# A hybrid decoder layer on one core: raw-weight tiles, the order of the experts, one expert's turn and the order of score products

## The chip, the cores and the metric

The kernel runs on one core of a Trainium2 chip. The metric is the device time of one execution in microseconds (us). TensorE, VectorE (DVE), ScalarE (ACT), GpSimd (POOL) and SyncE (SP, which issues most loads) each run their own list of instructions in order.

## The reference

One layer on 512 tokens of width 1024, all in f32: an input projection feeds four heads of chunked retention and eight heads of sliding-window attention; an output projection follows; then 32 experts, of which each token takes four; then a gated embedding and the last norm.

```python
hn = rmsnorm(h, g_mix_norm)
rq, rk, rv, rg, aq, ak, av = split_cols(hn @ w_in + b_in, IN_SIZES)
ret = silu(rg) * rmsnorm(retention(rq, rk, rv, positions), ret_norm_g)
att = sliding_window_attention(aq, ak, av, att_sinks, rel_bias_table)
h = h + concatenate([ret, att]) @ w_out
h = h + moe(rmsnorm(h, g_moe_norm), ...)   # per expert: clamped_swiglu(x @ w_up + b_up) @ w_down + b_down
gate = sigmoid(h @ w_ple_gate)
h = h + rmsnorm(gate * (p @ w_ple_proj), g_ple_norm)
return rmsnorm(h, g_final)
```

## The kernel before

**Weights.** All matrices of the later stages come as pieces of 1 MB (128 x 2048 f32), in one fixed list: w_out (4 pieces), then for each expert 8 pieces of w_up followed by the 4 pieces of w_down of the expert before it, then those of the end. A piece is loaded by SyncE into a raw tile taken from the list `free`, and a tile goes back there once its piece has been used or split. There are 12 raw tiles in three pools: `rawp` (3, there from the start), `raw2` (5, opened when attention and retention have been written down) and `raw3` (4, which first hold the mixed head outputs `mix` and come free tile by tile in the second half of the output projection). `next_piece` splits a piece into a high part `wh` on ScalarE (L150) and the rest `wl` on VectorE (L151), three tiles of each; a product of split operands takes three matmuls (`mm3`, L307 to L309). `whole_piece` uses a raw tile as it is.

**Stages.** Retention and attention run to about 212 us, woven into the products of the input projection (L315). Then the output projection goes over two halves of the columns and four token tiles in each (24 matmuls of 512 columns per tile and half, 192 in all), with transposes, router logits and top-4 after each tile (`route_tile`). Each token tile's normed rows `xn` go to the table xg in memory, from which every expert gathers its tokens (`gather`, L800). The expert stage follows from 297 to 1392 us.

**Experts.** They are sorted by how many tokens they have. The string `BIG` says for each rank whether it is handled big (L: up to 96 tokens, weights split, `up` at L847 and `down` at L928) or small (S: up to 64, weights straight from the raw tile, `up64` and `down64`, L864). Expert 0 and 1 are L. In the loop, the up products of expert e stand ahead of the down products of expert e - 1. The tokens of expert e + 1 are gathered two steps ahead, and turned (transposed on TensorE, copied by ScalarE into `xTh`: `prep` at L300, `prep64` at L815) right behind the up products of e, so ahead of the down products of e - 1. `act` computes the gated activation: Silu `sg` on ScalarE (L895), clamp and product on VectorE; `act_t` transposes it to `aTh`. `gated` scales the down result to `y`, and GpSimd scatters it into acc.

**Order.** A list scheduler orders each engine's instructions when the kernel is built, from the written order and its own estimates; `tc.issue_after` pins an instruction behind another.

Of the kernel before, what the change touches and what calls it, by code (L numbers as in the profile page):

```python
# [33 lines left out]
LIMIT = 7.0  # L34
S_MAX = float(ALPHA * LIMIT / (1.0 + math.exp(-ALPHA * LIMIT)))
CAP = 96
RAW1, RAW2, RAW3 = 3, 5, 4
FAR = 1000.0


# [3 lines left out]

BIG = [c == "L" for c in "LL" + "SLSLSLSLSLSLSLL" + "SLSLSLSLSLSLLLS"]
NBIG = sum(BIG)
RANK = [sum(BIG[:t]) if BIG[t] else NBIG + t - sum(BIG[:t]) for t in range(len(BIG))]
CAPS = 64  # L50
# [45 lines left out]
def hymba_kernel(ctx, tc, x, p, positions, rel_bias_table, g_mix_norm, w_in, b_in, ret_norm_g,  # L96
# [24 lines left out]
        return stack.enter_context(tc.tile_pool(name=name, bufs=bufs, reuse_waits="tile", **kw))  # L121

    const = pool(ctx, "const")
    rawp = pool(ctx, "rawp", RAW1)
    whp = pool(ctx, "whp", 3)
    wlp = pool(ctx, "wlp", 3)
    small = pool(ctx, "small", 3)
# [4 lines left out]


    R = SimpleNamespace(eid={})
    free = [rawp] * RAW1

    def raw_tile(dt=F32):
        pl_ = free.pop(0)
        return pl_.tile([P, 2048], dt, name="raw"), pl_

    def split(raw, parts=None, dst=None):
        if dst is None:
# [181 lines left out]

    px = ctx.enter_context(ExitStack())
    right = ctx.enter_context(ExitStack())
    raw3 = pool(ctx, "raw3", RAW3)
    mix = [raw3.tile([P, 2048], F32R, name="raw").rearrange("p (a k t) -> a p k t", a=2, k=KD) for _ in range(NT)]
    mm = pool(px, "mm", 2, PSUM)
    tp = pool(px, "tpp", 2, PSUM)  # L330
    sps = pool(px, "sps", 2, PSUM)
# [133 lines left out]
    def attention(nb):  # L465
        nk = 1 if nb == 0 else 2
        k0 = max(nb - 1, 0) * P
        o_sb = at2.tile([P, 512], F32, name="o_sb", bufs=1)
        o_ps = flat(oap.tile([P, 4, P], F32, name="o_ps")).rearrange("p (h d) -> p h d", d=64)
        sm = small.tile([P, 8], F32, name="sm")  # L470
        mx = small.tile([P, 8], F32, name="mx")
        nmx = small.tile([P, 8], F32, name="nmx")
        kvs = [slice(kv * 64, kv * 64 + 64) for kv in range(2)]
        for gp in range(2):

            s_ps = [sps.tile([P, 512], F32, name="s_ps").rearrange("p (a b) -> p a b", a=2) for _ in range(2)]
            for g in range(2):
                for kv, rows in enumerate(kvs):
                    nc.tensor.matmul(s_ps[kv][:, g, 0:nk * P], lhsT=aqT[rows, gp * 2 + g, nb * P:(nb + 1) * P],
                                     rhs=akT[rows, k0:k0 + nk * P], start=True, stop=True)  # L480
            for kv, rows in enumerate(kvs):
                h0 = kv * 4 + gp * 2
                h2_ = slice(h0, h0 + 2)
                s_sb = at2.tile([P, S], F32, name="s_sb").rearrange("p (a b) -> p a b", a=2)
                nc.vector.scalar_tensor_tensor(
                    s_sb[:, :, 0:nk * P], in0=s_ps[kv][:, :, 0:nk * P], scalar=0.125,
                    in1=band[:, h2_, 256 - nk * P:256], op0=ALU.mult, op1=ALU.add)
                nc.vector.tensor_reduce(out=mx[:, h2_], in_=s_sb[:, :, 0:nk * P], op=ALU.max, axis=AX.X)
# [124 lines left out]
    p1.close()  # L613


    raw2 = pool(right, "raw2", RAW2, side="right")
    rt = pool(right, "rt", side="right")
    free += [raw2] * RAW2

# [12 lines left out]
    for r0 in (0, 64):  # L632
        nc.gpsimd.memset(b_raw[r0:r0 + E, 0:1536], 0.0)
    nc.vector.scalar_tensor_tensor(R.bias, in0=b_hi[:, 0:1536].bitcast(F32), scalar=cst[:, C_SGN:C_SGN + 1],
                                   in1=b_raw[:, 0:1536], op0=ALU.mult, op1=ALU.add)
    state["limit"] = n_moe
    while free:
        prefetch()
# [99 lines left out]
    for c in range(2):  # L738
        cs = slice(c * 512, (c + 1) * 512)
        ws = {1: next_piece(), 0: next_piece()}  # L740
        for i in range(NT):
# [4 lines left out]
                mm3(ps, (mix[i][0][:, k, :], mix[i][1][:, k, :]), [kslice(w, k % 4) for w in ws[k // 4]],  # L746
                    k == order[0], k == order[-1])
            if c == 1:
                free.append(raw3)
                prefetch()  # L750
            nc.vector.tensor_tensor(out=h1[:, i, cs], in0=ps, in1=h1[:, i, cs], op=ALU.add)
            t = tp.tile([P, 4, P], F32, name="tp")
# [10 lines left out]
            if c == 0:  # L763
                nc.vector.tensor_copy(out=lg[:, i, :], in_=o)
            else:
                nc.vector.tensor_tensor(out=lg[:, i, :], in0=o, in1=lg[:, i, :], op=ALU.add)
                xn = tl.tile([P, D], F32, name="xn")
                for cc in range(2):
                    cs = slice(cc * 512, (cc + 1) * 512)
                    nc.gpsimd.tensor_tensor(out=xn[:, cs], in0=h1[:, i, cs], in1=g_moe[:, cs], op=ALU.mult)  # L770
                r = rstd(hs[i], None, 1)
                R.last_act = nc.scalar.activation(xn, xn, AF.Copy, scale=r)
                logits = tl.tile([P, E], F32, name="logits")
                nc.vector.scalar_tensor_tensor(logits, in0=lg[:, i, :], scalar=r, in1=b_rt, op0=ALU.mult, op1=ALU.add)
                nc.sync.dma_start(out=xg[tok, :], in_=xn)
                nc.sync.dma_start(out=acc[tok, :], in_=h1[:, i, :])
                route_tile(i, logits)


    def route(posm_ap, v_ap):  # L780
# [106 lines left out]

    def act(h):

        sg = R.sb.tile([P, FF], F32, name="sg", bufs=1)  # L890
        a = R.sb.tile([P, FF], F32, name="a", bufs=1)
        for v, h_ in enumerate(h):
            hv = h_.rearrange("p (c t) -> p c t", t=2)
            cs = slice(v * 512, (v + 1) * 512)
            nc.scalar.activation(sg[:, cs], hv[:, :, 0], AF.Silu, scale=ALPHA)  # L895
            nc.vector.tensor_scalar(a[:, cs], hv[:, :, 1], LIMIT + 1.0, 1.0 - LIMIT, op0=ALU.min, op1=ALU.max)  # L896
            R.act = nc.vector.scalar_tensor_tensor(a[:, cs], in0=sg[:, cs], scalar=S_MAX, in1=a[:, cs], op0=ALU.min,
                                                   op1=ALU.mult)
        return a

# [32 lines left out]
        return o  # L933

    def gated(o, gate):
        y = R.sb.tile([P, D], F32, name="y")
        nc.scalar.activation(y[:, 0:o.shape[1]], o, AF.Copy, scale=gate)  # L937
        return y

# [75 lines left out]

    def read_slots():

        tab = R.sb.tile([P, D], F32, name="y")[0:CAP, 0:8 * E].rearrange("p (k f) -> p k f", k=4)
        half = R.sb.tile([P, D], F32, name="y")[:, 0:E]
        for k in range(4):  # L1020
            nc.gpsimd.dma_start(out=tab[:, k, :], in_=slot_d[k].rearrange("(s e) c -> s (e c)", e=E))
        sums = slots.rearrange("p e c -> p (e c)")[0:CAP]
# [31 lines left out]
    for e in range(E + 1):  # L1054
        if e < E:
# [10 lines left out]
            if e == 0:  # L1066
                read_slots()
                static_gather(2)
            if e + 1 < E:
                with tc.issue_after(R.up_end.ins):  # L1070
                    xT = (prep if BIG[e + 1] else prep64)(xe[(e + 1) % 2])
        if e == E - 1:

            last = raw_tile()
# [16 lines left out]
        if e < E - 1:  # L1091
            with tc.issue_after(R.dn_mid.ins) if e else nullcontext():
                aT = act_t(a) if BIG[e] else act_t64(a)

    h2 = [t for _ in range(2) for t in raw_tile()[0].rearrange("p (a n) -> a p n", a=2)]
    proj = [t for _ in range(2) for t in raw_tile()[0].rearrange("p (a n) -> a p n", a=2)]
# [22 lines left out]
    with tc.If(any_v > 0), ExitStack() as sx:  # L1119
# [4 lines left out]
        for i in range(NT):  # L1124
            nc.gpsimd.dma_start(out=pos_d.rearrange("e p i -> p e i")[:, :, i], in_=posm[:, i, :])
            nc.gpsimd.dma_start(out=gate_d.rearrange("e p i -> p e i")[:, :, i], in_=gates[:, i, :])
        pe = ov.tile([P, NT], F32, name="pe")
        ge = ov.tile([P, NT], F32, name="ge")
        with tc.For_i(0, E, 1) as ev:
            n_e = nc.values_load(nblk[0:1, bass.ds(ev, 1)], min_val=0, max_val=NT)  # L1130
            nc.sync.dma_start(out=pe, in_=pos_d[bass.ds(ev, 1), :, :].rearrange("o p i -> p (o i)"))
# [2 lines left out]
            with tc.For_i(0, n_e, 1):  # L1134
# [7 lines left out]
                xd = R.sb.tile([P, D], F32, name="y")  # L1142
                nc.gpsimd.memset(xd, 0.0)
                gather(idx, xd, P)
                xTd = prep(xd)
# [32 lines left out]
    with tc.issue_after(ld.ins):  # L1178
        for _ in range(2):
            prefetch()  # L1180
    g_ple = bcast(ep2, g_ple_norm[0], D, "g_ple", nc.sync)
    g_fin = bcast(ep2, g_final, D, "g_fin", nc.sync)
    ws = [ws]
    free += [t[1] for t in (last, tmp, tf, tr)]
    hT = {}
    ss1 = {}

# [90 lines left out]
```

## Time and profile before

| | before |
|---|---|
| median of 3 runs | 1484.46 us (1481.01 to 1488.48) |
| profiled execution | 1485.38 us |
| its span | 1483.6 us |
| TensorE busy | 91% |
| VectorE busy | 56% |
| ScalarE busy | 46% |
| mean granted TensorE clock | 0.958 |
| memory traffic read | 447.26 MB |

The span is the traced part of the execution; 1.8 us lie around it. Busy shares are averages over stages that differ, so the text below goes by stage. A matmul's duration overlaps that of the next; its rate is read from the starts.

### The profile page before, as it was taken

To read this page: it belongs to the slowest core of one execution; us is meant where nothing else is said; L and a number is where in the kernel's file an instruction comes from. 1 tells how busy PE (TensorE), PEld (TensorE's weight loads), DVE (VectorE), ACT (ScalarE), POOL (GpSimd) and SP (SyncE) were. 2 spreads that over 40 slices of the span, in tenths; PEclk is the share of its full clock that TensorE was granted. 3 is DMA by queue.
4 is the path that set the end of the run, shared out by engine and by line. 5 is a ranking of instruction groups with operands and counts; after the bars stand their busy time and mean duration, and the time that the engine had idled before them with its cause. 6 is when DMAs were issued, how large, how long until landed. Compare 5 with 4: busy or idle time off the path is not lost. (4 is left out here: it accounts for less than half of the span.)

```text
span 1483.6 us, 16861 instructions
## 1 busy us (share of the span) xinstructions
PE 1351.3 (91%) x6090; PEld 907.1 (61%) x6091; DVE 830.1 (56%) x1005; ACT 677.7 (46%) x750; POOL 224.4 (15%) x238
## 2 busy tenths in 40 slices
PE   5999999588999999999999999999999999999885
PEld 4777777466657474655647657465655647675564
DVE  6637774776547263544637647354553726683356
ACT  5333443455536253543626535343452625573443
POOL 2213241474100000000000000000100000000023
PEclk9999999788999999999999999999999999999998
DMA  9332046667899999999999999999999999987511
GB/s 272 118 109 58 29 142 254 237 254 280 318 402 396 403 405 396 406 399 393 392 396 408 393 388 387 375 403 396 386 394 399 395 387 400 391 328 283 183 72 43
DMA packets 110427, 462.47 MB, mean 312 GB/s; under 512 B 10830, under 2 KB 29180, under 8 KB 77568
## 3 DMA queue, kind: packets, MB, share of 16 engines
q1 hardware_dynamic: 99584, 436.24, 74.8%
q0 software_dynamic: 10320, 24.52, 6.5%
q8 instruction: 49, 0.80, 0.2%
q10 hardware_dynamic: 432, 0.57, 0.1%
q14 instruction: 42, 0.34, 0.1%
HBM read 447.26 MB, written 18.73 MB: 314 GB/s over the span
## 5 line engine op out<-in xcount | busy, mean ns | idle before, releaser
L151 DVE TENSOR_TENSOR wl<-raw,wh 128x2048 fp32r<-128x2048 f32 (+2 forms) x243 | 530.2, 2222 | 151.8 <-ACT wh L150 143.8
L150 ACT ACTIVATE wh<-raw 128x2048 fp32r<-128x2048 f32 (+2 forms) x243 | 442.9, 1858 | 110.2 <-PE up L847 52.2
L864 PE MATMUL up<-raw,xTh 128*64 128x512 f32 x896 | 195.3, 594 | 0.0
L896 DVE TENSOR_SCALAR a<-up 128x512 f32<-128x512 f32 x50 | 32.9, 687 | 267.8 <-ACT sg L895 267.8
L847 PE MATMUL up<-wh,xTh 128*128 128x512 f32 x576 | 162.8, 405 | 9.2 <-ACT wh L150 7.8
L895 ACT ACTIVATE sg<-up 128x512 f32<-128x512 f32 x50 | 27.9, 595 | 297.0 <-issue 158.5
L847 PE MATMUL up<-wl,xTh 128*128 128x512 f32 x576 | 160.9, 401 | 2.2 <-DVE wl L151 2.2
L847 PE MATMUL up<-wh,xTl 128*128 128x512 f32 x576 | 161.0, 401 | 1.4 <-DVE xTl L292 1.4
L864 PEld LDWEIGHTS up<-raw,xTh 128*64 128x64 f32 x896 | 63.1, 137 | 124.6 <-issue 120.0
L847 PEld LDWEIGHTS up<-wh,xTh 128*128 128x128 f32 x576 | 108.7, 191 | 40.5 <-ACT wh L150 13.1
L847 PEld LDWEIGHTS up<-wl,xTh 128*128 128x128 f32 x576 | 109.0, 191 | 32.8 <-DVE wl L151 7.0
L847 PEld LDWEIGHTS up<-wh,xTl 128*128 128x128 f32 x576 | 109.8, 191 | 28.2 <-DVE xTl L292 1.8
L928 PE MATMUL dn<-wh,aTh 128*128 128x512 f32 x288 | 100.8, 434 | 23.8 <-ACT wh L150 23.8
L928 PE MATMUL dn<-wl,aTh 128*128 128x512 f32 x288 | 104.0, 446 | 15.9 <-DVE wl L151 15.9
L942 POOL DMA_INDIRECT acc<-y,slot_i x30 | 45.4, 1514 | 443.3 <-ACT y L937 434.8
L800 POOL DMA_INDIRECT xe<-xg,slot_i x30 | 31.9, 1064 | 485.9 <-PE dn L857 261.0
L864 PE MATMUL dn<-raw,aT 128*64 128x512 f32 x448 | 102.9, 598 | 0.0
L928 PE MATMUL dn<-wh,aTl 128*128 128x512 f32 x288 | 98.2, 425 | 0.0
L928 PEld LDWEIGHTS dn<-wh,aTh 128*128 128x128 f32 x288 | 59.4, 211 | 42.8 <-ACT wh L150 27.3
L928 PEld LDWEIGHTS dn<-wl,aTh 128*128 128x128 f32 x288 | 58.5, 212 | 35.5 <-DVE wl L151 23.1
L914 DVE SCALAR_TENSOR_TENSOR aTl<-tp,aTh 128x512 fp32r<-128x512 f32 x36 | 24.1, 689 | 90.2 <-ACT aTh L913 90.2
L928 PEld LDWEIGHTS dn<-wh,aTl 128*128 128x128 f32 x288 | 59.3, 206 | 15.0
(340 smaller groups left out, 1571.9 us busy)
## 6 DMA issues: line engine op xcount, KB each, us to landing
raw<-in_w_up_dram SPq DMA_DIRECT2D x256, 1024.0 KB, 17.4
raw<-in_w_down_dram SPq DMA_DIRECT2D x128, 1024.0 KB, 17.9
raw<-in_w_in_dram SPq DMA_DIRECT2D x32, 256.0 KB, 4.8
raw<-in_w_out_dram SPq DMA_DIRECT2D x4, 1024.0 KB, 5.0
raw<-in_w_ple_gate_dram SPq DMA_DIRECT2D x4, 1024.0 KB, 10.4
raw<-in_w_in_dram SPq DMA_DIRECT2D x3, 1024.0 KB, 5.7
xt<-in_x_dram SPq DMA_DIRECT2D x4, 512.0 KB, 6.5
h<-in_x_dram POOLq DMA_DIRECT2D x4, 512.0 KB, 7.6
```

What stands on the lines that cost most here:

```text
L150: R.split_act = nc.scalar.activation(to(wh), src(raw), AF.Copy)
L151: R.split_dve = nc.vector.tensor_tensor(out=to(wl), in0=src(raw), in1=to(wh).bitcast(F32), op=ALU.subtract)
L800: return nc.gpsimd.indirect_dma_start(out=dst[0:n, 0:D // h], out_offset=None, in_=xg.rearrange("s (h d) -> (s h) d", h=h), in_offset=bass ...
L847: nc.tensor.matmul(h[n // 2][:, n % 2 * 512:n % 2 * 512 + 512], lhsT=a[:, k, :], rhs=w[:, n * 512:(n + 1) * 512], start=(k == 0 and a is x ...
L864: R.pair = nc.tensor.matmul(o[v * 64:v * 64 + 64, c:c + 512], lhsT=xT[:, k, :], rhs=w[:, v * n + c:v * n + c + 512], start=False, stop=las ...
L895: nc.scalar.activation(sg[:, cs], hv[:, :, 0], AF.Silu, scale=ALPHA)
L896: nc.vector.tensor_scalar(a[:, cs], hv[:, :, 1], LIMIT + 1.0, 1.0 - LIMIT, op0=ALU.min, op1=ALU.max)
L914: nc.vector.scalar_tensor_tensor(flat(l[:, g4, :]), in0=flat(t), scalar=1.0 / ALPHA, in1=flat(h[:, g4, :]).bitcast(F32), op0=ALU.mult, op1 ...
L928: m = nc.tensor.matmul(o[:, n * 512:(n + 1) * 512], lhsT=a[:, k, :], rhs=w[:, kk * 1024 + n * 512:kk * 1024 + (n + 1) * 512], start=False, ...
L942: nc.gpsimd.indirect_dma_start(out=acc.rearrange("s (h d) -> (s h) d", h=h), out_offset=bass.IndirectOffsetOnAxis(ap=idx[0:n, :], axis=0), ...
```

## The change

There are 13 raw tiles instead of 12 (`RAW2` 6). Their room comes from elsewhere: the two tiles for `xn` are now raw tiles, `sg` is half as long with one buffer, `y` and some tiles of the overflow path lose a buffer, and two gains of the end lie in a raw tile. Each raw tile has a place of its own (a tag). The order of the last 15 ranks changes from SLSLSLSLSLSLLLS to SLSLSLLSLLSLLSS. The turn of the third expert's tokens (written at e = 1) moves behind the first expert's down products. In attention, the four score products of a pass are pinned one behind the other, so that the two key heads alternate.

```diff
-RAW1, RAW2, RAW3 = 3, 5, 4
+RAW1, RAW2, RAW3 = 3, 6, 4
...
-BIG = [c == "L" for c in "LL" + "SLSLSLSLSLSLSLL" + "SLSLSLSLSLSLLLS"]
+BIG = [c == "L" for c in "LL" + "SLSLSLSLSLSLSLL" + "SLSLSLLSLLSLLSS"]
...
+    free = [(rawp, f"a{j}") for j in range(RAW1)]
+
+    def raw_tile(dt=F32, name="raw"):
+        place = free.pop(0)
+        return place[0].tile([P, 2048], dt, name=name, tag=place[1], bufs=1), place
...
+            m = None
             for g in range(2):
                 for kv, rows in enumerate(kvs):
-                    nc.tensor.matmul(s_ps[kv][:, g, 0:nk * P], lhsT=aqT[rows, gp * 2 + g, nb * P:(nb + 1) * P],
-                                     rhs=akT[rows, k0:k0 + nk * P], start=True, stop=True)
+                    with tc.issue_after(m.ins) if m is not None else nullcontext():
+                        m = nc.tensor.matmul(s_ps[kv][:, g, 0:nk * P], lhsT=aqT[rows, gp * 2 + g, nb * P:(nb + 1) * P],
+                                             rhs=akT[rows, k0:k0 + nk * P], start=True, stop=True)
...
-    free += [raw2] * RAW2
+    free += [(raw2, f"b{j}") for j in range(RAW2)]
...
+    xns = [raw_tile(F32, "xn") for _ in range(2)]
     state["limit"] = n_moe
     while free:
         prefetch()
...
-                xn = tl.tile([P, D], F32, name="xn")
+                xn = xns[i % 2][0][:, 0:D]
...
+    for t in xns:
+        free.append(t[1])
+        prefetch()
...
-        sg = R.sb.tile([P, FF], F32, name="sg", bufs=1)
...
-            nc.scalar.activation(sg[:, cs], hv[:, :, 0], AF.Silu, scale=ALPHA)
+            sg = R.sb.tile([P, 512], F32, name="sg", bufs=1)
+            nc.scalar.activation(sg, hv[:, :, 0], AF.Silu, scale=ALPHA)
...
-        y = R.sb.tile([P, D], F32, name="y")
+        y = R.sb.tile([P, D], F32, name="y", bufs=1)
...
+            def turn():
+                return (prep if BIG[e + 1] else prep64)(xe[(e + 1) % 2])
+
+            if e + 1 < E and e != 1:
                 with tc.issue_after(R.up_end.ins):
-                    xT = (prep if BIG[e + 1] else prep64)(xe[(e + 1) % 2])
+                    xT = turn()
...
                 aT = act_t(a) if BIG[e] else act_t64(a)
+        if e == 1:
+            xT = turn()
...
-    g_ple = bcast(ep2, g_ple_norm[0], D, "g_ple", nc.sync)
-    g_fin = bcast(ep2, g_final, D, "g_fin", nc.sync)
+    g_ple, g_fin = last[0][:, 0:D], last[0][:, D:2 * D]
```

SyncE's loads at the output projection; before, two pieces of w_out stand ahead of every w_up piece:

```order
L170 DMA raw<-in_w_in_dram 128x4x128 x24
L156 DMA raw<-in_w_out_dram 128x4x512 x2
L186 DMA raw<-in_w_up_dram 128x2048 x3
L156 DMA raw<-in_w_out_dram 128x4x512 x2
L186 DMA raw<-in_w_up_dram 128x2048 x6
```

And after:

```order
L171 DMA raw<-in_w_in_dram 128x4x128 x24
L187 DMA raw<-in_w_up_dram 128x2048
L157 DMA raw<-in_w_out_dram 128x4x512 x4
L187 DMA raw<-in_w_up_dram 128x2048 x7
L780 DMA acc<-h_2014 128x1024
```

All four w_out pieces now stand together behind one w_up piece.

TensorE at the same place, before; `mm<-wl,act_h` is the last of the input projection, `tp<-cst,y` ends a retention group, and `mm<-wh,raw` is the output projection:

```order
L315 MATMUL mm<-wl,act_h 128x512 x4
L307 MATMUL mm<-wh,raw 128x512
L308 MATMUL mm<-wh,raw 128x512
L309 MATMUL mm<-wl,raw 128x512
...
L598 MATMUL tp<-cst,y 128x128 x2
L555 MATMUL tp<-cst,ra 128x128 x4
L307 MATMUL mm<-wh,raw 128x512
L308 MATMUL mm<-wh,raw 128x512
```

And after:

```order
L316 MATMUL mm<-wl,act_h 128x512 x4
L601 MATMUL tp<-cst,y 128x128 x2
L558 MATMUL tp<-cst,ra 128x128 x4
L575 MATMUL s_ps<-qkT 128x128
L583 MATMUL s_ps<-vs,ra 128x128
L578 MATMUL or_ps<-vs,sc 128x128
L580 MATMUL or_ps<-r_prev,qkT 128x128
...
L601 MATMUL tp<-cst,y 128x128 x2
L308 MATMUL mm<-wh,raw 128x512
```

The last retention group runs through without products of the output projection between its own.

TensorE behind the second expert's up products, before; `tp<-cst,xe` is the turn of the third expert's tokens:

```order
L834 MATMUL up<-bias,sel 128x512 x4
L815 MATMUL tp<-cst,xe_2004 128x128 x4
L834 MATMUL dn<-bias,sel 128x512 x2
L928 MATMUL dn<-wh,aTh 128x512 x2
...
L911 MATMUL tp<-cst,a 128x128 x8
L857 MATMUL up<-bias,sel_3272 128x512 x2
L864 MATMUL up<-raw,xTh 64x512 x32
```

And after:

```order
L841 MATMUL up<-bias,sel 128x512 x4
L841 MATMUL dn<-bias,sel 128x512 x2
L935 MATMUL dn<-wh,aTh 128x512 x2
...
L918 MATMUL tp<-cst,a 128x128 x8
L864 MATMUL up<-bias,sel_3284 128x512 x2
L822 MATMUL tp<-cst,xe_2004 128x128 x4
L871 MATMUL up<-raw,xTh 64x512 x32
```

The turn stands behind the first expert's down products and the second expert's activations.

TensorE in the last attention pass, before; `s_ps<-akT,aqT` are the score products:

```order
L572 MATMUL s_ps<-qkT 128x128
L479 MATMUL s_ps<-akT,aqT 128x256 x2
L575 MATMUL or_ps<-vs,sc 128x128
L577 MATMUL or_ps<-r_prev,qkT 128x128
L479 MATMUL s_ps<-akT,aqT 128x256 x4
L315 MATMUL mm<-wl,act_h 128x512
L479 MATMUL s_ps<-akT,aqT 128x256 x2
```

And after:

```order
L575 MATMUL s_ps<-qkT 128x128
L482 MATMUL s_ps<-akT,aqT 128x256
L316 MATMUL mm<-wh,act_l 128x512
L578 MATMUL or_ps<-vs,sc 128x128
L580 MATMUL or_ps<-r_prev,qkT 128x128
L482 MATMUL s_ps<-akT,aqT 128x256 x3
```

Of each four, one now stands alone and three together.

ScalarE's list holds 16 table loads after the change and 14 before; the last of attention and retention, after:

```order
L566 ACT_TABLE_LOAD
L566 ACTIVATE gt<-u 128x256
L496 ACT_TABLE_LOAD
L496 ACTIVATE s_sb,sm<-s_sb,nmx 128x256 x4
L510 ACTIVATE es<-es 128x8
...
L593 ACTIVATE y,ss_1790<-or_ps,cst 128x128 x2
L566 ACT_TABLE_LOAD
```

Before, the same exponentials had one load ahead of them and the `gt` behind them one more.

## Rows read from the trace of the kernel before

**Rows 1.** Stretches: busy us (instructions) of each engine, TensorE clock, DMA share, rate.
```profile
130.00:212.70 82.70, 79.27 (x443) 61.34 (x442) 60.52 (x159) 40.83 (x99) 20.46 (x33) 1.00 0.19 61
...
229.30:278.00 48.70, 45.23 (x233) 35.67 (x233) 26.36 (x83) 17.34 (x30) 13.05 (x30) 1.00 0.68 255
...
420.00:1300.00 880.00, 833.03 (x3623) 519.16 (x3621) 456.26 (x302) 400.38 (x336) 66.41 (x52) 0.96 1.01 395
1300.00:1392.00 92.00, 86.29 (x387) 56.69 (x385) 52.95 (x37) 46.14 (x40) 4.29 (x3) 1.00 0.71 263
```

**Rows 2.** TensorE in time, 596 to 664: start, duration, work, [idle before it, releaser].
```profile
647.43 0.73 PE L928 MATMUL dn<-wh,aTh 128*128 128x512 f32 x2 [2.16 <-ACT wh L150]
...
649.75 1.22 PE L928 MATMUL dn<-wl,aTh 128*128 128x512 f32 x2 [1.13 <-DVE wl L151]
```

**Rows 3.** ScalarE in time, the same stretch.
```profile
643.90 0.60 ACT L895 ACTIVATE sg<-up 128x512 f32<-128x512 f32 x1 [13.30 <-issue]
...
645.46 5.51 ACT L150 ACTIVATE wh<-raw 128x2048 fp32r<-128x2048 f32 x3
```

**Rows 4.** The line of the w_down loads, 600 to 650: issues and landing.
```profile
L192 SPq DMA_DIRECT2D raw<-in_w_down_dram x4: 372/383/560, 623.0 to 629.1; - x4
...
DMA to landing us min/median/max: 18.2/20.3/21.2
```

**Rows 5.** TensorE in time where a big expert follows a big one, 826 to 836.
```profile
832.70 1.85 PE L847 MATMUL up<-wh,xTh 128*128 128x512 f32 x4 [2.76 <-ACT wh L150]
```

**Rows 6.** TensorE in time around the third expert's turn, 350 to 378.
```profile
355.05 0.73 PE L834 MATMUL up<-bias,sel 64*128 64x512 f32 x4
361.33 1.09 PE L815 MATMUL tp<-cst,xe 128*128 128x128 f32 x4 [5.55 <-DMA xe<-xg,slot_i]
...
376.83 1.51 PE L864 MATMUL up<-raw,xTh 128*64 128x512 f32 x6
```

**Rows 7.** ScalarE in time, the same place.
```profile
362.46 0.60 ACT L816 ACTIVATE xTh<-tp 128x512 f32<-128x512 f32 x1 [5.35 <-PE tp L815]
...
376.95 1.11 ACT L937 ACTIVATE y<-dn,ig 128x1024 f32<-128x1024 f32 x1
377.94 1.09 ACT L913 ACTIVATE aTh<-tp 128x512 fp32r<-128x512 f32 x2
378.90 0.42 ACT L855 ACTIVATE sel<-same,sel 128x128 fp32r<-128x128 f32 x1
```

**Rows 8.** SyncE's queue in time, 100 to 235 (a row's time runs to its last issue).
```profile
126.66 45.45 SPq L156 DMA_DIRECT2D raw<-in_w_out_dram  x2
```

**Rows 9.** ScalarE in time, 185 to 240.
```profile
196.46 1.28 ACT L563 ACT_TABLE_LOAD   x1 [0.88 <-DVE es L508]
197.75 0.42 ACT L563 ACTIVATE gt<-u 128x256 f32<-128x256 f32 x1
...
203.69 1.91 ACT L150 ACTIVATE wh<-raw 128x2048 fp32r<-128x2048 f32 x1
```

**Rows 10.** VectorE in time, 185 to 234.
```profile
201.85 1.81 DVE L634 SCALAR_TENSOR_TENSOR bias<-wh,cst,raw 128x1536 fp32r<-128x1536 f32 x1
...
206.60 2.28 DVE L151 TENSOR_TENSOR wl<-raw,wh 128x2048 fp32r<-128x2048 f32 x1
```

**Rows 11.** TensorE in time at the start of the output projection, 205 to 232.
```profile
212.72 0.40 PE L307 MATMUL mm<-wh,raw 128*128 128x512 f32 x1
212.95 0.40 PE L308 MATMUL mm<-wh,raw 128*128 128x512 f32 x1
...
227.43 0.41 PE L598 MATMUL tp<-cst,y 128*128 128x128 f32 x2 [1.04 <-DVE y L595]
```

**Rows 12.** TensorE in time, 140 to 186: score products (two records each).
```profile
143.96 0.70 PE L479 MATMUL s_ps<-akT,aqT 64*128 64x256 f32 x2
...
181.47 1.13 PE L479 MATMUL s_ps<-akT,aqT 64*128 64x256 f32 x4
...
183.17 1.34 PE L479 MATMUL s_ps<-akT,aqT 64*128 64x256 f32 x8
```

More of the change, by code (lines that the diff above doesn't have):

```diff
@@ L123, in hymba_kernel @@
     const = pool(ctx, "const")
-    rawp = pool(ctx, "rawp", RAW1)
+    rawp = pool(ctx, "rawp")
     whp = pool(ctx, "whp", 3)
@@ L134, in hymba_kernel @@
     R = SimpleNamespace(eid={})
[L135 to L139, printed above, removed]
+    free = [(rawp, f"a{j}") for j in range(RAW1)]
+    def raw_tile(dt=F32, name="raw"):
+        place = free.pop(0)
+        return place[0].tile([P, 2048], dt, name=name, tag=place[1], bufs=1), place
     def split(raw, parts=None, dst=None):
@@ L326, in hymba_kernel @@
     right = ctx.enter_context(ExitStack())
-    raw3 = pool(ctx, "raw3", RAW3)
-    mix = [raw3.tile([P, 2048], F32R, name="raw").rearrange("p (a k t) -> a p k t", a=2, k=KD) for _ in range(NT)]
+    raw3 = pool(ctx, "raw3")
+    mix = [raw3.tile([P, 2048], F32R, name="raw", tag=f"c{j}", bufs=1).rearrange("p (a k t) -> a p k t", a=2, k=KD) for j in range(NT)]
     mm = pool(px, "mm", 2, PSUM)
@@ L613, in hymba_kernel @@
     p1.close()
-    raw2 = pool(right, "raw2", RAW2, side="right")
+    raw2 = pool(right, "raw2", side="right")
     rt = pool(right, "rt", side="right")
-    free += [raw2] * RAW2
+    free += [(raw2, f"b{j}") for j in range(RAW2)]
     b_raw, b_pool = raw_tile()
@@ L748, in hymba_kernel @@
             if c == 1:
-                free.append(raw3)
+                free.append((raw3, f"c{i}"))
                 prefetch()
@@ L894, in act @@
             cs = slice(v * 512, (v + 1) * 512)
-            nc.scalar.activation(sg[:, cs], hv[:, :, 0], AF.Silu, scale=ALPHA)
+            sg = R.sb.tile([P, 512], F32, name="sg", bufs=1)
+            nc.scalar.activation(sg, hv[:, :, 0], AF.Silu, scale=ALPHA)
             nc.vector.tensor_scalar(a[:, cs], hv[:, :, 1], LIMIT + 1.0, 1.0 - LIMIT, op0=ALU.min, op1=ALU.max)
-            R.act = nc.vector.scalar_tensor_tensor(a[:, cs], in0=sg[:, cs], scalar=S_MAX, in1=a[:, cs], op0=ALU.min,
+            R.act = nc.vector.scalar_tensor_tensor(a[:, cs], in0=sg, scalar=S_MAX, in1=a[:, cs], op0=ALU.min,
                                                    op1=ALU.mult)
@@ L1016, in read_slots @@
     def read_slots():
-        tab = R.sb.tile([P, D], F32, name="y")[0:CAP, 0:8 * E].rearrange("p (k f) -> p k f", k=4)
-        half = R.sb.tile([P, D], F32, name="y")[:, 0:E]
+        tab = R.sb.tile([P, D], F32, name="y", bufs=1)[0:CAP, 0:8 * E].rearrange("p (k f) -> p k f", k=4)
+        half = R.sb.tile([P, KD, 64], F32, name="aT64", bufs=1)[:, 0, 0:E]
         for k in range(4):
@@ L1068, in hymba_kernel @@
                 static_gather(2)
-            if e + 1 < E:
+            def turn():
+                return (prep if BIG[e + 1] else prep64)(xe[(e + 1) % 2])
+            if e + 1 < E and e != 1:
                 with tc.issue_after(R.up_end.ins):
-                    xT = (prep if BIG[e + 1] else prep64)(xe[(e + 1) % 2])
+                    xT = turn()
         if e == E - 1:
@@ L1126, in hymba_kernel @@
             nc.gpsimd.dma_start(out=gate_d.rearrange("e p i -> p e i")[:, :, i], in_=gates[:, i, :])
-        pe = ov.tile([P, NT], F32, name="pe")
-        ge = ov.tile([P, NT], F32, name="ge")
+        pe, ge = t_f[:, 1024:1024 + NT], t_f[:, 1032:1032 + NT]
         with tc.For_i(0, E, 1) as ev:
@@ L1141, in hymba_kernel @@
                 idx, gate = route(pe.rearrange("p (i o) -> p i o", o=1), v)
-                xd = R.sb.tile([P, D], F32, name="y")
+                xd = R.sb.tile([P, D], F32, name="xd", bufs=1)
                 nc.gpsimd.memset(xd, 0.0)
@@ L1180, in hymba_kernel @@
             prefetch()
-    g_ple = bcast(ep2, g_ple_norm[0], D, "g_ple", nc.sync)
-    g_fin = bcast(ep2, g_final, D, "g_fin", nc.sync)
+    g_ple, g_fin = last[0][:, 0:D], last[0][:, D:2 * D]
+    for dst, src in ((g_ple, g_ple_norm[0]), (g_fin, g_final)):
+        nc.sync.dma_start(out=dst, in_=src.rearrange("(o n) -> o n", o=1).broadcast_to([P, D]))
     ws = [ws]
-    free += [t[1] for t in (last, tmp, tf, tr)]
+    free += [t[1] for t in (tmp, tf, tr)]
     hT = {}
```

## The prediction

> **What bounds the kernel now.** I read the table of stretches first [rows 1]. In the expert stage TensorE is busy for 833.03 of 880 us while the DMA share is 1.01, so both look full; the waits decide. I take one pair of a small and a big expert and ask what TensorE waits for: 2.16 us for a ScalarE split and 1.13 us for the VectorE half of it [rows 2]. The ScalarE rows of the same stretch show why [rows 3]: the Silu at 643.90 stands ahead of the splits in ScalarE's order, it needs the up products that end there, and ScalarE idles 13.30 us before it. The weights are not late: the first of the four loads was issued at 623.0 and landed at most 21.2 us on, by 644.2 [rows 4], the split began at 645.46. So the stage is bound by TensorE, and its 47 us of gaps (880 less 833.03) are mostly the order on ScalarE. Where a big expert follows a big one behind a small one, the wait is 2.76 us [rows 5].
>
> Before the experts TensorE is also nearly full: 79.27 of 82.70 us up to 212.7 and 45.23 of 48.70 us in the output projection [rows 1]. Work taken out of those stretches shortens the run; work pushed back out of the stretch 212.7 to 229.3 lengthens it.
>
> **The change part by part,** against the profiled run (1485.38 us, of which 1483.6 are the span; 0.92 us above the median 1484.46).
>
> *Third expert's turn.* After the last up product of the second expert (355.05, 0.73 us) TensorE stands 5.55 us until the rows of the third have been gathered [rows 6]. The first down products, whose tokens and weights are there, stand behind that. After the change they go first, and the turn comes behind them, when the rows have been there for some 8 us. What remains of it: before, the third expert's up products began at 376.83. After, the down products begin 5.55 us earlier plus the 1.09 us of the turn's four transposes, so they end near 369. Then ScalarE has in its order the scaled result 1.11, the second expert's activations 1.09, the selector 0.42 and only then the tokens, 0.60 [rows 7]: 369.0 + 3.2 = 372.2 with the copies back to back, so the up products begin at about 372.3. Gain 4.5 us; bounds 2.5 (ScalarE late by another copy and a half) and 5.55 (nothing of it paid again). It carries through, as the experts behind are bound by TensorE.
>
> *Output projection.* The two tiles for xn now come out of the raw pool. Before, two pieces of w_out were loaded into raw tiles that had come free early (first issue 126.66; the second follows 45.45 us later [rows 8]), and split at 203.69 on ScalarE and 206.60 on VectorE [rows 9, 10]. So when the last input-projection product was through, TensorE went on with w_out products at 212.72, one each 0.23 us [rows 11], in the gaps of the last retention group, whose transposes at 227.43 wait 1.04 us for VectorE. I count 45 of the stage's 192 products up to 229.3: 45 x 0.233 = 10.5 us of cover. After, the first three raw tiles go to the bias table and xn, all four w_out loads go to the newly opened pool, behind a w_up load that waits for the bias (201.85 + 1.81 [rows 10]), and the ScalarE splits stand behind the last retention group's copies. TensorE has nothing to put under that group's chain. The sum: the 45 products come later, +10.5; the chain from the last input product to the last transposes (14.7 us before) is shorter by the nine w_out products inside it, -2.1, and no longer behind a 2.28 us split on VectorE, of which I take -1; the first split can begin only after the chain, +2 to 3 (1.91 for ScalarE's part [rows 9], then the wait for VectorE's 2.28), less about 1 that hides under the products that need only the first half. That is +8.4 to +9.4; of TensorE's 3.5 idle us between 229.3 and 278 (48.70 less 45.23) some may absorb a part. I take +9. Ends: +12.5 (10.5 + 3 - 1, the chain no shorter), and +3, if the stage is paced by the router's chain behind it and the delay disappears there.
>
> *Score products.* Before, one product of a head pair alone takes 0.70 us in its two records, two in the same rows 1.13, four of which the middle two alternate 1.34 [rows 12]. After, each group of four is one product, something else, then three in alternation (0.70 + about 1.0 = 1.7). The blocks with the order 2, 4, 2 (3.60 us) become 3.4; the block whose last six stood singly (1.13 + 6 x 0.70 = 5.3) becomes about 4. Two blocks of the first kind and one of the second: -2 us, bounds -2.3 and 0.
>
> *ScalarE's tables.* The new order puts two more table loads into the last attention and retention, 1.28 us each [rows 9]. The Trainium skill, page "ScalarE: Activation LUTs", section "What ACT_TABLE_LOAD costs", puts a drain of about 1.38 us beside the load, 2.66 in all, and so speaks against this order: by it the two would occupy 5.3 us instead of 2.6. In the row the activation follows at 197.75, right at the end of the load, so no drain shows behind it here. ScalarE is not full there and TensorE has fill products: +1, bounds 0 and +2.6.
>
> *Two small experts last.* From the eighteenth on, the order has one big-after-small wait (2.16 + 1.13 = 3.3 us [rows 2]) fewer but two more of 2.76 [rows 5]: +2.2. The end with two small experts has plain down products, no split on ScalarE, and gives back about 1 of the 5.7 idle us after 1300 [rows 1]. The weights can follow: the DMA share falls to 0.71 there. +1, bounds -5 and +6.
>
> *The 13th buffer.* The loads land before the splits ask for them [rows 3, 4], and the DMA engines are at 1.01 already: 0, bounds -3 and 0. The half-size sg buffer makes ScalarE's second Silu wait for VectorE; ScalarE copies the next tokens meanwhile, and TensorE wants the activations only after the next up products: 0. One y buffer: the next result comes a whole expert later: 0.
>
> Sum: -4.5 + 9 - 2 + 1 + 1 + 0 = +4.5, **1485.4 + 4.5 = 1490 us.**
>
> **The rivals.** *The projection absorbs the delay.* If the stage 229 to 278 is paced by softmax, masks and router logits on VectorE and not by the products, the lost cover costs 3 instead of 9, and with the last experts at -2: 1485.4 - 4.5 + 3 - 2 - 2 = 1480; with the last experts at -5, 1477. For it: TensorE is not quite full there. Against: 45.23 of 48.70 us.
>
> *The buffer closes the bubbles.* The same gap returns in every pair, and one more tile lets loads run further ahead. If a third of the 47 us closed, the time would be 1490 - 15.7 = 1474. Against it [rows 3, 4]: ScalarE idle with data there. The Trainium skill, "Perfetto Trace Analysis", section "Identifying Performance Opportunities", reads a gap that repeats on the engine that should be full as a possible sign of too few buffers; by that rule this case would be the likeliest. The trace gives the order on ScalarE instead.
>
> *The closing stage speeds up.* Two small experts need no split; if all 5.7 us of idle time after 1300 go and the projection absorbs half its delay (+4.5), the time is 1485.4 - 4.5 + 4.5 - 2 + 1 - 5.7 = 1479.
>
> *The cover is missed in full.* Slower than before: the w_out loads come so late that TensorE stands through the whole chain and then through two splits (+12.5), table loads delay the last attention (+2.6), and the waits of the last experts are 3 more: 1485.4 + 12.5 + 2.6 + 4 - 4.5 - 1 = 1499. It decides from the point at which the first w_out product starts after about 228 on the old clock.
>
> *The turn does not pay.* ScalarE has four things ahead of the third expert's tokens; if the earlier down products also outrun the splits of their last weights, only 2.5 us are won: 1492.
>
> **How the numbers follow.** Forecast with its bounds (1484 to 1493): 0.40. Projection absorbs: 0.16. Buffer: 0.07. Closing stage: 0.12. Cover missed in full: 0.17. Turn doesn't pay: 0.08. 0.5% is 7.4 us, about what a measurement of this kernel tells from no change: faster is below 1477, slower above 1491.9. Faster: the buffer, half of the other two fast cases: 0.21. Slower: cover missed, three quarters of the turn case, a fifth of the forecast: 0.31. Same: 0.48. The range from 1474 to 1499 leaves a tenth out at either end.
>
> **What would show it.** The w_out products start at 225 to 230 in place of 212.7, with TensorE mostly idle in the ten us before; the last products of that stage end 6 to 8 us later than 277. No gap of 5 us behind the second expert's up products, and the third's up products nearer to it by 4.5. The gap at each big-after-small step stays 3.3 us with 13 buffers. If those gaps shrink, the buffer theory was right; if the first expert's products begin no later than at 299, the cost of the projection was wrong; if the run ends 10 us sooner behind the same last up products, the closing stage was.

## The result and the profile after

The changed kernel takes 1493.44 us (median, 1491.95 to 1494.76) beside 1485.28 us: a ratio of 1.0052, with an interval of 1.0035 to 1.0068. That is 8 us slower; 1490 had been forecast. The profiled execution has a span of 1492.6 us.

The stretches of [rows 1] in the changed kernel (busy us and instructions of TensorE, its weight loads, VectorE, ScalarE and GpSimd, then TensorE's clock, the DMA share and GB/s), with two more, 212.7 to 229.3 and 278 to 297, that show where the loss begins:

```profile
212.70:229.30 16.60, 6.07 (x22) 4.64 (x22) 9.46 (x29) 3.55 (x9) 7.32 (x11) 0.64 0.74 256
229.30:278.00 48.70, 45.83 (x217) 36.02 (x217) 19.32 (x40) 18.17 (x27) 5.47 (x7) 0.91 0.58 218
278.00:297.00 19.00, 15.52 (x85) 12.06 (x84) 14.08 (x55) 6.11 (x13) 9.84 (x26) 0.97 0.75 255
420.00:1300.00 880.00, 836.96 (x3651) 533.58 (x3650) 485.22 (x318) 424.53 (x349) 67.09 (x53) 0.96 1.00 391
1300.00:1392.00 92.00, 87.00 (x375) 49.39 (x373) 37.42 (x24) 31.45 (x28) 2.87 (x2) 0.98 0.82 315
```

The same two further stretches before:

```profile
212.70:229.30 16.60, 14.15 (x72) 10.73 (x70) 11.00 (x31) 3.92 (x13) 8.42 (x11) 1.00 0.76 275
278.00:297.00 19.00, 4.10 (x40) 3.37 (x40) 12.52 (x41) 9.86 (x12) 8.89 (x13) 0.55 0.59 211
```

From 212.7 to 229.3 TensorE does 22 things where it did 72 before, and its mean granted clock there is 0.64 in place of 1.00: part of the stretch runs at 1.2 GHz, which no part of it did before. TensorE in time at that place (start, duration, work, idle time before it and its releaser), beside [rows 11]:

```profile
217.80 0.66 PE L601 MATMUL tp<-cst,y 128*128 128x128 f32 x2 [5.56 <-DVE y L598]
...
223.80 0.63 PE L580 MATMUL or_ps<-r_prev,qkT 128*128 128x128 f32 x2
228.79 0.66 PE L601 MATMUL tp<-cst,y 128*128 128x128 f32 x2 [4.36 <-DVE y L598]
232.25 0.79 PE L308 MATMUL mm<-wh,raw 128*128 128x512 f32 x1 [2.80 <-ACT wh L151]
```

The output projection begins at 232.25, in place of 212.72. Its last product starts at 292.8 (277.0 before), and the first expert's tokens are turned at 312.4 (297.0 before). SyncE and ScalarE at the same place, beside [rows 8, 9]:

```profile
207.79 22.61 SPq L157 DMA_DIRECT2D raw<-in_w_out_dram  x4
```

```profile
230.30 3.70 ACT L151 ACTIVATE wh<-raw 128x2048 fp32r<-128x2048 f32 x2
237.16 1.92 ACT L151 ACTIVATE wh<-raw 128x2048 fp32r<-128x2048 f32 x1 [3.17 <-DMA raw<-in_w_out_dram]
```

The first w_out load is issued 81 us later than before, and the first split stands behind the last copy of the retention group.

The third expert's turn, TensorE, ScalarE and VectorE, beside [rows 6, 7]:

```profile
369.01 0.73 PE L935 MATMUL dn<-wh,aTh 128*128 128x512 f32 x2
...
384.94 1.11 PE L822 MATMUL tp<-cst,xe 128*128 128x128 f32 x4 [3.12 <-DVE aTl L921]
386.74 5.54 PE L871 MATMUL up<-raw,xTh 128*64 128x512 f32 x14 [0.69 <-ACT xTh L823]
```

```profile
381.86 1.10 ACT L944 ACTIVATE y<-dn,ig 128x1024 f32<-128x1024 f32 x1
382.86 1.08 ACT L920 ACTIVATE aTh<-tp 128x512 fp32r<-128x512 f32 x2
```

```profile
384.20 1.28 DVE L921 SCALAR_TENSOR_TENSOR aTl<-tp,aTh 128x512 fp32r<-128x512 f32 x2
```

The 5.55 us are gone, and 3.12 + 0.69 us stand in their place: the turn's transposes wait for a transpose buffer that VectorE still reads for the second expert's activations.

### The profile page after: what moved, and what is told of

Its sections match the earlier page's. It is cut to its first block, busy times and chain, and to the rows that moved or that the text cites. A ratio compares the mean times of both kernels' runs of the same rounds, so it can differ in the third digit from the quotient of the medians.

```text
span 1492.6 us, 16889 instructions
## 1 busy us (share of the span) xinstructions
PE 1358.5 (91%) x6090; PEld 909.5 (61%) x6091; DVE 831.3 (56%) x1003; ACT 683.6 (46%) x754; POOL 222.7 (15%) x238
## 5 line engine op out<-in xcount | busy, mean ns | idle before, releaser
L871 PE MATMUL up<-raw,xTh 128*64 128x512 f32 x896 | 199.0, 600 | 0.7 <-ACT xTh L823 0.7
L944 ACT ACTIVATE y<-dn,slots 128x1024 f32<-128x1024 f32 (+1 forms) x30 | 27.5, 916 | 90.5 <-PE dn L935 51.9
```

The lines of the kernel that those rows point to most:

```text
L871: R.pair = nc.tensor.matmul(o[v * 64:v * 64 + 64, c:c + 512], lhsT=xT[:, k, :], rhs=w[:, v * n + c:v * n + c + 512], start=False, stop=las ...
```

## The experiments

All medians are device us; the kernel before had 1485.6 to 1488.4 beside them.

**xn in the new pool.** The changed kernel, w_out in the early tiles again:

```diff
-    xns = [raw_tile(F32, "xn") for _ in range(2)]
+    xpl = [free.pop() for _ in range(2)]
+    xns = [(q[0].tile([P, 2048], F32, name="xn", tag=q[1], bufs=1), q) for q in xpl]
```

> The changed kernel, but the two xn tiles are taken from the end of the list of free raw tiles (the newly opened pool), so that w_out gets the two early tiles again. Theory (the place of xn costs the cover of the output projection, and the idle chain costs the clock): the output projection starts at about 212 again, the clock stays at 1.00 from 212.7 to 229.3, the first expert's up products begin at 298 to 300 in place of 314.5, and the time is 1493.4 - 15 = 1478. Rival (the two more table loads and the pinned score products delay the chain): the first expert still begins at 310 to 315 and the time stays within 3 us of 1493.

1480.06 us, 13.4 less than the changed kernel. The output projection begins at 212.3, the first expert's tokens are turned at 300.1. The stretches:

```profile
212.70:229.30 16.60, 14.41 (x66) 11.81 (x66) 10.57 (x28) 4.28 (x11) 8.95 (x12) 0.90 0.71 277
278.00:297.00 19.00, 3.36 (x40) 2.62 (x40) 12.44 (x41) 9.86 (x12) 8.79 (x13) 0.62 0.90 316
```

The place of xn was the cause of the late start. The second row shows a smaller cost: the DMA share ahead of the experts is 0.90 (0.59 in the same stretch of the kernel before), and the first gather, issued at 287.7, ends TensorE's wait only 12.5 us later, where it took 8.3 before (288.75 to 297.05). The share alone is not the cause: in the repaired kernel with 12 tiles (below) it is 0.96, and the gather takes 8.1 us (286.66 to 294.80). What lengthens it stays open.

**Score products alone.** The kernel before with the pinned order:

```diff
+                    with tc.issue_after(m.ins) if m is not None else nullcontext():
+                        m = nc.tensor.matmul(s_ps[kv][:, g, 0:nk * P], ...)
```

> The kernel before with the score products pinned in alternation and nothing else. Theory (prediction): -2 for the products, +1 for two more table loads, so 1484 beside 1485.3; the first expert begins 0 to 2 us earlier. Rival (the pinning moves the last attention late and takes the fill): the first expert begins 4 us or more later and the time is 1489 or more.

1478.89 us, ratio 0.9959 (0.9939 to 0.9978): 6.7 us less, more than forecast. The last input product starts at 210.3 in place of 212.5, as forecast; the first expert's tokens are turned 4.2 us earlier. In the changed kernel the same products, beside [rows 12]:

```profile
145.12 0.70 PE L482 MATMUL s_ps<-akT,aqT 64*128 64x256 f32 x4
...
185.22 1.13 PE L482 MATMUL s_ps<-akT,aqT 64*128 64x256 f32 x6
```

Two products that alternate take the 0.70 us of one, three the 1.13 us of two in the same rows.

**Turn alone.**

```diff
-            if e + 1 < E:
+            if e + 1 < E and e != 1:
...
+        if e == 1:
+            xT = turn()
```

> The kernel before with the third expert's turn behind the first down products and nothing else. Prediction: 4.5 us less, 1480.8. Theory from the changed trace (the turn waits for a transpose buffer that VectorE frees behind the second expert's activations, and the clock falls in that wait): the gap of 5.5 us gives way to one of 3 to 4, the third expert's up products begin 2 to 5 us earlier but run at the lower clock for a while, and 1 us or less is left: 1484.5.

1484.01 us, ratio 0.9983 (0.9966 to 1.0000). Little is left, as the second theory has it; the gaps are 3.14 and 0.69 us, as in the changed kernel.

**Order alone.**

```diff
-"SLSLSLSLSLSLLLS"
+"SLSLSLLSLLSLLSS"
```

> The kernel before with the new order of the last 15 experts and nothing else. Prediction: +1, 1486. Theory from the changed trace (from the nineteenth expert to the end of the experts it took 4 us longer): +4, 1489. If it is the order together with the 13th buffer that took the time, this kernel is within 1 us of 1485.3.

1492.95 us, ratio 1.0041 (1.0022 to 1.0059): 7.4 us more. One of its two new steps in which a big expert follows a big one behind a small one, TensorE in time:

```profile
1081.02 1.71 PE L847 MATMUL up<-wh,xTh 128*128 128x512 f32 x4 [2.75 <-ACT wh L150]
1082.53 1.91 PE L847 MATMUL up<-wh,xTl 128*128 128x512 f32 x4
```

Behind the wait four products take 1.91 us, where they take 1.10 elsewhere: TensorE is at 1.2 GHz for a while (its granted clock is 0.57 from 1081 to 1085). This trace also has a turn of the third expert that waited 11.48 us in place of 5.55:

```profile
366.15 1.08 PE L815 MATMUL tp<-cst,xe 128*128 128x128 f32 x4 [11.48 <-DMA xe<-xg,slot_i]
```

**Buffer alone.** The changed kernel with the old order, the old turn and unpinned score products (the diff of the change without these three parts).

> The changed kernel without its other three parts: 13 raw tiles with xn in two of them and the shorter sg and y buffers, but the old order of experts, the old turn and the score products unpinned. Theory (xn in the early raw tiles costs 13 to 15 us before the experts, and the 13th buffer gives back some 7 us among them, as the changed trace against the order alone suggests): first expert at 312 to 315, time 1492 to 1494. Rival (the prediction's: the buffer is worth nothing among the experts): 1485.5 + 14 = 1499 or more.

1490.26 us, ratio 1.0033 (1.0014 to 1.0052): below both theories. The first expert's tokens are turned at 309.7 (12.7 later), but the experts take 1002 us from the third on where they took 1016 (table below).

**The clock kept.** The changed kernel with transposes that nothing reads, in the last retention group:

```diff
             t = tp.tile([P, 4, P], F32, name="tp")
+            for _ in range(40 if h == 3 and i0 == 2 else 0):
+                nc.tensor.transpose(out=t[:, 2, :], in_=ident, identity=ident)
```

> The changed kernel with 40 more transposes of the identity, whose result nothing reads, in the last retention group, so that TensorE is not idle while it waits there. Theory (the idle chain costs the clock, and the first output-projection products run at half of it until about 237): the clock is back at 1.00 when those products begin at about 232, and the first expert begins 2 to 3 us earlier, at 312, the time is 1491. Rival (the clock there costs nothing, since the splits pace those products): first expert at 314 to 315, 1493.4 unchanged.

1496.79 us, 3.4 more than the changed kernel; the intervals of the two ratios, 1.0058 to 1.0099 and 1.0035 to 1.0068, overlap. The stretches of this kernel around the start of the output projection:

```profile
229.00:232.00 3.00, 0.41 (x2) 0.20 (x2) 1.32 (x4) 1.20 (x3) 0.00 (x0) 0.96 0.22 12
232.00:235.00 3.00, 1.80 (x4) 1.49 (x5) 1.82 (x1) 2.95 (x2) 0.00 (x0) 0.50 0.92 343
235.00:238.00 3.00, 3.00 (x8) 1.99 (x7) 2.95 (x3) 1.92 (x1) 0.00 (x0) 0.50 1.10 418
```

It did not test what it was made for. The transposes brought the clock back, but the wait for the first split behind them stayed, and it fell again to 0.50 for the same products. The first product starts at 233.2, 1 us later. Where the rest of the 3.4 us comes from, if it is a difference at all, stays open, and so does what the lower clock costs there.

**Repaired.** xn in the new pool, the old order, and the turn ahead of the second expert's activations:

```diff
+        if e == 1:
+            xT = turn()
         if e < E - 1:
             with tc.issue_after(R.dn_mid.ins) if e else nullcontext():
                 aT = act_t(a) if BIG[e] else act_t64(a)
-        if e == 1:
-            xT = turn()
```

> The changed kernel with three repairs: xn in the new pool's tiles, the old order of experts, and the third expert's turn ahead of the second's activations. If the parts add up (1480.1 with xn moved, -7 for the order, -2 for the turn): 1471. If the 13th buffer is worth something only with the new order: 1478 or more.

1469.44 us, ratio 0.9895 (0.9874 to 0.9916): the parts add up.

**The same without the buffer's part:** the kernel before, score products pinned, turn as in the repaired kernel.

> The kernel before with the score products pinned and the third expert's turn behind the first down products and ahead of the second expert's activations: the same as the repaired kernel but with 12 raw tiles. Parts added up: 1478.9 - 4 = 1475. Theory (the 13th buffer is worth some 7 us among the experts): 4 to 8 us slower than the repaired kernel. Rival (it is worth nothing): within 2 us of it.

1471.37 us, ratio 0.9898 (0.9878 to 0.9918): the rival, the whole part is worth 2 us.

**The repaired kernel with 12 tiles.**

```diff
-RAW1, RAW2, RAW3 = 3, 6, 4
+RAW1, RAW2, RAW3 = 3, 5, 4
```

> The repaired kernel with one raw tile less in the new pool (12 instead of 13) and nothing else changed, so the shorter sg and y buffers stay. Theory (the 13th tile itself shortens the experts, as the traces of all kernels with 13 have a pair of experts in 64.9 us where those with 12 alternate between 65.9 and 67.2): the experts take 8 us or more longer from the third on, pairs of 66 to 67 us, and the gather ahead of them is at most 3 us shorter: 1474 to 1478. Rival (it is sg, y and the order that follows from them, or the phase of the clock): pairs of 64.9 us as with 13, time within 2 us of 1469.

1471.05 us, ratio 0.9901 (0.9877 to 0.9925). The pairs of a small and a big expert take 65.6 to 67.2 us again, as the theory had it, where most take 64.9 with 13 tiles, but the times differ by only 1.6 us, as the rival had it. A big expert's down products behind a small expert, with 13 tiles:

```profile
944.74 1.15 PE L936 MATMUL dn<-wh,aTh 128*128 128x512 f32 x2 [2.11 <-ACT wh L151]
945.70 1.05 PE L936 MATMUL dn<-wh,aTl 128*128 128x512 f32 x2
947.07 1.22 PE L936 MATMUL dn<-wl,aTh 128*128 128x512 f32 x2 [0.32 <-DVE wl L152]
```

And with 12, otherwise the same kernel:

```profile
944.98 0.73 PE L936 MATMUL dn<-wh,aTh 128*128 128x512 f32 x2 [2.11 <-ACT wh L151]
...
947.30 0.86 PE L936 MATMUL dn<-wl,aTh 128*128 128x512 f32 x2 [1.13 <-DVE wl L152]
947.96 1.06 PE L936 MATMUL dn<-wh,aTh 128*128 128x512 f32 x2
```

The first wait, 2.11 us, is the same. With 13 tiles TensorE is at the lower clock as soon as the products begin (1.05 us for two that take 0.63 elsewhere), while it has to wait for the splits anyway; with 12 it first runs, waits 1.13 us, and slows down then. The length of a pair goes with this and not with the number of tiles. The kernel without the buffer's part has 12 tiles and two pairs of 64.9 and 65.0 us among longer ones; these begin slow, like this one:

```profile
569.67 1.17 PE L930 MATMUL dn<-wh,aTh 128*128 128x512 f32 x2 [2.16 <-ACT wh L150]
```

Buffer alone has 13, and its pairs up to 795 take 65.8 to 67.1; these begin fast:

```profile
595.14 0.73 PE L933 MATMUL dn<-wh,aTh 128*128 128x512 f32 x2 [2.11 <-ACT wh L151]
```

**Waits filled.** The repaired kernel, with transposes into columns that the next product overwrites:

```diff
         with tc.issue_after(R.up_end.ins), tc.issue_after(R.rows_end.ins):
+            for _ in range(16 if e + 1 < E and not BIG[e + 1] else 0):
+                nc.tensor.transpose(out=o[:, 0:P], in_=ident, identity=ident)
...
         h = [up_tile(), up_tile()]
+        for _ in range(20 if e > 2 and BIG[e - 1] and not BIG[e - 2] else 0):
+            with tc.issue_after(R.at.ins):
+                nc.tensor.transpose(out=h[1][:, 512:640], in_=ident, identity=ident)
```

> The repaired kernel with transposes of the identity, whose results are written over, in TensorE's waits: 16 ahead of the bias of a big expert's down products behind a small expert (the 2.1 us gap), 20 where a big expert follows a big one behind a small one (the 2.76 us gap). Theory (a wait of 2 us costs its own time and then a stretch of some 3.5 us at the lower clock, so 1.7 us more for each of 16): the clock from 420 to 1300 goes from 0.97 to 0.99 or more, and the time falls by 10 to 25 us, to 1445 to 1459. Rival (the products behind the gap are paced by the splits, and the clock costs nothing there): within 2 us of 1469, or slower by what the transposes hold up.

1457.34 us, ratio 0.9802 (0.9779 to 0.9825): 12 us less than the repaired kernel, for work that computes nothing.

**Waits filled, 12 tiles:** the same in the kernel without the buffer's part.

> The kernel with 12 raw tiles, pinned score products and the early turn (1471.4), with the same transposes in TensorE's waits. Theory of the clock: 10 to 25 us less, 1446 to 1461; if with 12 tiles the phase of the clock made the pairs longer, this one gains more than the one with 13 tiles and the two end within 3 us of each other. Rival: 1471 unchanged.

1454.53 us, ratio 0.9788 (0.9765 to 0.9811): 17 us less than without, the fastest of all. The stretch of the experts in the kernel without the buffer's part, then in this one:

```profile
420.00:1300.00 880.00, 834.27 (x3635) 520.58 (x3632) 465.76 (x309) 410.16 (x341) 65.31 (x51) 0.96 1.01 394
```

```profile
420.00:1300.00 880.00, 852.13 (x3932) 542.21 (x3929) 481.50 (x316) 424.82 (x351) 66.83 (x52) 1.00 1.01 398
```

TensorE in time in this kernel, the two kinds of wait:

```profile
809.34 2.35 PE L847 MATMUL up<-cst 128*128 128x128 f32 x20
812.26 1.20 PE L852 MATMUL up<-wh,xTh 128*128 128x512 f32 x4 [0.57 <-ACT wh L150]
```

```profile
931.13 1.91 PE L927 MATMUL dn<-cst 128*128 128x128 f32 x16
...
933.89 0.74 PE L935 MATMUL dn<-wh,aTh 128*128 128x512 f32 x2 [0.43 <-ACT wh L150]
```

The products start no earlier for it: 2.35 + 0.57 us stand where 2.76 were, and 1.91 + 0.43 where 2.1 were. They run at 2.4 GHz behind it, and that is the gain.

**The new order, waits filled.** The last kernel with the order SLSLSLLSLLSLLSS.

> The kernel with 12 raw tiles, pinned score products, the early turn and TensorE's waits filled (1454.5), but with the new order of the last 15 experts. In kernels with open waits the new order cost 7 us. Theory (two thirds of that is the lower clock behind the two more waits of 2.76 us; with the waits filled it is gone): 0 to 3 us more, 1455 to 1458. Rival (the new order is slower by its work or by its splits, whatever the clock): 1460 or more.

1457.40 us, ratio 0.9796 (0.9774 to 0.9818) beside 0.9788: the two intervals overlap almost entirely, so no cost of the order can be told apart here. The time is where the theory put it, but how much of the order's cost was the clock behind its waits it does not show: that cost alone had an interval of 3 to 9 us.

From the traces of all kernels, one profiled run each (the experts' times scatter by some 4 us between runs of one kind; the profiled runs of repaired and of the first filled, 12 lie 4 and 5 us below the medians of their kernels, that of the last row 4 above), where the experts begin and how long they take:

| kernel | tiles, order | first tokens turned | third's up begins | last down ends | third to end |
|---|---|---|---|---|---|
| before | 12, old | 297.0 | 376.8 | 1392.4 | 1015.6 |
| scores alone | 12, old | 292.8 | 372.2 | 1386.6 | 1014.4 |
| turn alone | 12, old | 296.3 | 372.9 | 1391.7 | 1018.8 |
| no buffer | 12, old | 294.4 | 365.4 | 1378.3 | 1012.9 |
| repaired, 12 | 12, old | 294.8 | 366.7 | 1377.5 | 1010.8 |
| order alone | 12, new | 297.7 | 382.3 | 1404.3 | 1022.0 |
| buffer alone | 13, old | 309.7 | 392.4 | 1394.8 | 1002.4 |
| repaired | 13, old | 299.9 | 370.9 | 1372.3 | 1001.4 |
| changed | 13, new | 312.4 | 386.7 | 1401.3 | 1014.6 |
| xn in the new pool | 13, new | 300.1 | 373.8 | 1388.0 | 1014.2 |
| clock kept | 13, new | 313.4 | 385.1 | 1399.3 | 1014.2 |
| filled | 13, old | 298.8 | 370.0 | 1364.8 | 994.8 |
| filled, 12 | 12, old | 292.3 | 361.2 | 1360.1 | 998.9 |
| filled, 12 | 12, new | 294.5 | 365.6 | 1368.4 | 1002.8 |

## Why the prediction was right, and where not

The time lies in the range and on the forecast side, 3.4 us above the forecast. But the sum came near by luck, because its errors cancelled: two costs (output projection, order) were too small, the gain of the turn was too large, and two gains (score products, buffer) were too small. Alone, the four parts measured +4.6 (the buffer with the place of xn), +7.4, -6.7 and -1.6, together +3.7 where the change as a whole measured +8.2; with intervals of nearly 3 us to either side for each, the difference is not told from chance.

**Output projection, +9 forecast.** The mechanism was right, the term mis-sized: the experts begin 15.4 us later, and moving xn back gives 13.4. The step that failed is "the chain from the last input product to the last transposes is shorter" (-2.1 and -1). It took 17.0 us (211.8 to 228.8) in place of 14.9 (212.5 to 227.4). Without the woven-in products and the splits it still waited 5.56 and 4.36 us for VectorE, whose norm stands between, and the group's own products ran at the lower clock, which the idle TensorE had fallen to (0.50 from 220 to 223):

```profile
220.00:223.00 3.00, 2.82 (x10) 2.27 (x10) 1.01 (x4) 0.11 (x1) 0.00 (x0) 0.50 0.96 283
```

From the first transposes to the last of these products it is 6.0 us (217.80 to 223.80), with no w_out product between. Before, it was 4.7, with the nine between:

```profile
217.32 0.41 PE L598 MATMUL tp<-cst,y 128*128 128x128 f32 x2 [0.94 <-DVE y L595]
...
222.04 0.39 PE L577 MATMUL or_ps<-r_prev,qkT 128*128 128x128 f32 x2
```

Nothing was absorbed later either: the stage ended 15.8 us later. The first product came 3.5 us behind the last transposes, where 2 to 3 had been put down. It comes close to the rival "the cover is missed in full", whose mark, a start after 228, was met with 232.25.

**Turn, -4.5 forecast.** Alone -1.6, with an interval that just reaches 0. Three things went past the working. It took the copies on ScalarE as the chain, and missed that the turn's transposes need a buffer that VectorE's `aTl` frees: 3.12 us. It put down nothing for the clock behind that wait: the third expert's 64 up products take 2.5 us longer in the turn alone than before (granted clock 0.85 in place of 1.00), and that takes back most of the 3.2 us by which they begin sooner behind the first turn.

```profile
372.86 16.47 PE L864 MATMUL up<-raw,xTh 128*64 128x512 f32 x64 [0.69 <-ACT xTh L816]
```

Before:

```profile
376.83 13.95 PE L864 MATMUL up<-raw,xTh 128*64 128x512 f32 x64
```

And the wait it removes is not one number: 5.55 us in the trace of before, 9.27, 11.48 and 11.28 in those of scores alone, order alone and buffer alone, which keep the old turn. From the first turned tokens to the third expert it is 79 to 85 us with the old turn, 72 to 77 with the new, 69 to 72 with the turn ahead of the activations, as the table gives it; there the turn is worth 7.5 us (scores alone 1478.89, no buffer 1471.37).

**Score products and table loads, -2 and +1 forecast.** Alone -6.7. The input projection ends 2.2 us earlier, as the sum said. Some 2 us more come before the experts (4.2 in all), the rest in the experts and after them, within what single runs scatter by; what the pinned order does to the other engines' order there was not taken apart. The table loads cost nothing that shows, and the rows show no drain behind a load: the row at 213.25 in the changed kernel has its activation right behind it. Nor does one show ahead of a load: the load at 173.24 in the kernel before stands right behind the activation ahead of it.

```profile
213.25 1.28 ACT L566 ACT_TABLE_LOAD   x1 [2.27 <-DVE rs_w L278]
214.54 0.42 ACT L566 ACTIVATE gt<-u 128x256 f32<-128x256 f32 x1
```

```profile
171.73 1.49 ACT L631 ACTIVATE wh<-raw 128x1536 fp32r<-128x1536 f32 x1 [0.87 <-issue]
173.24 1.28 ACT L563 ACT_TABLE_LOAD   x1
174.53 0.42 ACT L563 ACTIVATE gt<-u 128x256 f32<-128x256 f32 x1
```

That is how the prediction weighed the Trainium skill, "ScalarE: Activation LUTs", section "What ACT_TABLE_LOAD costs": its 1.28 us agree with the row, the drain that it adds shows neither behind a load nor ahead of one.

**Order, +1 forecast.** Alone +7.4. The waits were counted right: one of 3.3 us less, two of 2.76 us more. A missing term is the lower clock behind each of them, but it is not shown to be the whole. From the up products at 832.70 [rows 5] to the last down product it is 559.7 us before and 565.6 in order alone (from 838.70), 5.9 more; with the waits filled it is 547.8 and 551.5, and 3.7 are left. Another 4.8 us of the trace of order alone lie ahead of the third expert, where its rows came late, and are not the order's. The rest stays open. The closing stage did not speed up either, as one rival had it: from 1300 to 1392 TensorE idles 5.0 us where it idled 5.7.

**The 13th buffer, 0 forecast.** The reason given holds: the wait at the splits is 2.11 us with 12 and with 13 tiles. The Trainium skill ("Perfetto Trace Analysis", section "Identifying Performance Opportunities") gives too few buffers as what a gap that repeats can mean, which the prediction named as a rival; here the gap is ScalarE's order, and a further buffer left it as it was. In the traces the experts do take less: 9 us between the repaired kernels with 13 and 12 tiles. Of that, 5 are lost ahead of the experts, where the first gather takes 11.8 us (288.16 to 299.94) in place of 8.1, and the medians differ by 1.6, which their intervals do not tell from nothing. The shorter pairs are those that begin at the lower clock, with either number of tiles, and with the waits filled five of nine pairs take 64.3 or 64.4 us in both kernels. So the pairs are shorter by where the lower clock falls. Why it falls there more often with 13 tiles stays open.

## What to carry to other kernels

Ask of every buffer that moves what its place did early in the program: two tiles given to xn took the cover from a stretch that begins 30 us ahead of their first use (212.7 and 242.3). Price a wait of TensorE as the wait and the products behind it at the lower clock; where the wait cannot go, work that computes nothing can be worth more than a better order. And read a wait that ends with a gather from several runs, not from one.

## What had not been expected of the hardware

Behind waits of 2.1 to 2.8 us TensorE ran some 3 us of products at 1.2 GHz (two products in 1.05 us in place of 0.63, four in 1.91 in place of 1.10), in some pairs only after a second wait of 1.1 us. With 16 transposes of 128 columns in the wait (1.91 us) the products behind it ran at 2.4 GHz: the granted clock of the expert stage went from 0.97 to 1.00 with 13 tiles and from 0.96 to 1.00 with 12, and 12 and 17 us with it. Score products of 64 rows that alternate between the halves run beside each other: two in 0.70 us, the time of one.
